# A hybrid streaming encoder layer: causal masks on DVE, and another order at the stage boundary, in the interleaved units and at the end

## The chip, the core and the metric

One core of a Trainium2 chip runs the whole layer as one program. The metric is the device time of one execution in microseconds (us). Five engines work side by side, each through its own queue in order: TensorE (PE, with its weight loads shown as PEld), VectorE (DVE), ScalarE (ACT), GpSimd (POOL) and SyncE (SP), which here issues all DMAs of the program.

## What is computed

One layer on 2048 prompt frames and 32 frames of a running stream with 512 cached rows, all in float32. A projection is split among two mixers: a state-space scan (SSD) and a forgetting attention (FoX) with 16 heads of 64. The attention part and the end are what the change touches:

```
def fox_attend(q, k, v, fq, fk, q_pos, k_pos):
    s = jnp.einsum('bqhd,bkhd->bhqk', q, k, preferred_element_type=jnp.float32) * ATTN_SCALE
    s = s + jnp.swapaxes(fq, 1, 2)[:, :, :, None] - jnp.swapaxes(fk, 1, 2)[:, :, None, :]
    s = jnp.where((k_pos[None, :] <= q_pos[:, None])[None, None], s, -jnp.inf)
    p = jax.nn.softmax(s, axis=-1)
    return jnp.einsum('bhqk,bkhd->bqhd', p.astype(v.dtype), v)
...
    y_attn = o.reshape(bsz, t, D_ATTN).astype(f32) * jax.nn.silu(z_attn.astype(f32))
    mixed = jnp.concatenate([y_ssm, y_attn], axis=-1).astype(x.dtype) @ w_out
    h = ALPHA * x.astype(f32) + mixed.astype(f32)
    ... layer norm of h
```

## The kernel before, in words

Products that need more than one pass of precision are made of a high and a low part (`hi`/`lo`, `xh`/`xl`, `yh`/`yl`), three matmuls for one product.

**Projections and SSD (until about 1384 us).** The input projection runs channel tile by channel tile. In its last part 24 jobs (8 each for q, k and z of the attention, list `jobs`) of five column blocks (`BL`) are interleaved with the steps of the SSD scan by `at(n, ...)`. Each block ends in `tile_q`, `tile_k` or `tile_z`, which write their results to DRAM (q and k as a high and a low half, z through SiLU). From here on the matmuls are held in program order (`strict`, `mm`).

**The boundary.** During the last job the SBUF of the SSD is given back (`sx.close()`), and `begin()` (at block `b == RB`) opens the pools of the next stage on the right side: `w_begin` loads the eight tiles of the output weight that the SSD half needs (`w_request`), and `more()` splits them into high and low (`w_split`). The rest of the last job's outputs go through tiles of the new pools (`ux`, `uh`, `ul`). When the last job is done the memory of the input is free, and the attention's pools are opened (`a0`, `aq`, `ap`).

**Attention, three streams in one.** For each of 8 head pairs `p` and 4 query blocks `g` of 512:

- the *max stream* (`maxima`): per step one block `r` of 128 queries against one block `c` of 512 keys, two heads; a matmul `mp<-k,qa`, and on DVE `tensor_tensor_reduce` (L725, `jk`), which takes the gate `fb` off and keeps the running maximum `mx`. In the diagonal block (`c == g`) a second matmul (`mp<-trq,idb`, bf16) adds the causal mask. Two PSUM buffers (`pmx`, `MB = 2`), shared with `turn` (`pm`, the transposed maxima) and `total` (`sum`).
- the *value stream* (`values`): per step `j` 128 keys against 512 queries, two heads: `s<-qa,k` and `s<-qb,k`, in the four diagonal steps a mask matmul `s<-trb,idb`, then the exponential on ACT (L791, `pr`), the running sum `acc` on POOL (L798), and two steps later the product with the values (`po<-pr,va`), every second step eight matmuls at once. There are 320 such steps, 128 of them diagonal.
- the *units* (`ssm_proj`): the SSD half of the output projection, 272 units of three matmuls (`u<-wh,uh` and two more). Eight units make one row of 128 frames; a row needs four tiles of 256 KB (`uh`, `ul`, a ring of `UB = 3` each).

The streams are woven by hand in the loop at the end of the stage: first `U0 = 8` units, then `L0 = 22` steps of the max stream with two units after each, then one value step at a time; after each value step come a max step, the `chores` (`turn`, `split`), the units that are due, a step of the sample stream and `finish_steps` (`total` and the rest of the normalisation of an earlier block).

**The end.** When the values are done, `finish_steps` closes the last block of the attention, while `products` starts on the attention half of the output projection with the first three tiles of frames (`first`); their rows 0 to 3 of eight are there early, 4 to 6 are requested with `rows`, row 7 needs the last block. Then tile 16 and tiles 3 to 15 follow; each has products, the residual, and a layer norm on DVE, ACT and POOL. `y_next` holds the split rows of the next tile.

What is not pinned or held by `strict` is placed by the scheduler of the tile framework, by priority and free buffers; `pin` keeps an instruction in program order on its queue.

Of the kernel before, what the change touches and what calls it, by code (L numbers as in the profile page):

```python
# [19 lines left out]
ND = 32  # L20
# [7 lines left out]
KB, K2B, VB, FB, QA, QB, L0, LEAD, U0, RB, S0 = 6, 4, 4, 4, 4, 3, 22, 22, 8, 2, 2  # L28
# [3 lines left out]
def hymba_step(  # L32
# [220 lines left out]
    def gates():  # L253
# [28 lines left out]
        one = g2.tile([16, 1], F32, name="one")  # L282
        V.memset(one, 1.0)
# [3 lines left out]
        def scan(out, d, initial=0.0):  # L287
            V.tensor_tensor_scan(out=out, data0=one.to_broadcast([16, out.shape[1]]), data1=d, initial=initial,
                                 op0=ALU.mult, op1=ALU.add)
# [72 lines left out]
    with tc.tile_pool(name="tp", bufs=2) as tp, tc.tile_pool(name="wt", bufs=2, side="right") as wtp:  # L362
        for i in range(8):
            hi, lo = load_w(w_tok[i], 256, wtp)
            if i == 7:
                w_first = load_w(w_ch[28], 128)
# [148 lines left out]
    k2t, ws, w_steps, w_raw = [], [], [], []  # L515
# [31 lines left out]

    def qt(kind, dtype=F32R):
        if len(qpool) == 1:
            return qpool[0].tile([128, TB], dtype, name=kind, bufs=1 if kind == "f" else 2)  # L550
        if kind == "f":
            return qpool[1].tile([128, 512], F32, tag="ux", name="ux", bufs=1)
        t = qpool[1].tile([128, 4, 128], F32R, tag="u" + kind, name="u" + kind, bufs=UB)
        return t.rearrange("p a b -> p (a b)")

    if True:
# [32 lines left out]
        jobs = [(i, fn, p) for p in range(8) for i, fn in [(2, tile_z), *qk]]  # L589
# [16 lines left out]
        def begin():  # L606
            ex = tc.tile_pool(name="ep", bufs=1, side="right")
# [3 lines left out]
            right.extend([ex, fx, wx, px])  # L611
            right.extend([x.__enter__() for x in (ex, fx, wx, px)])
            k2t.extend(right[4].tile([66, 2, 512], F32R, name=f"k2{i}") for i in range(K2B))
            for i in range(K2B):
                GP.memset(k2t[i][64:66].bitcast(F32), 1.0)
            qpool.append(right[6])
            w_begin(right[6])

        def more():
            for _ in range(3):  # L620
                next(w_steps[0], None)
# [3 lines left out]
        for j, (i, fn, p) in enumerate(jobs):  # L625
# [3 lines left out]
            for b, (t0, m) in enumerate(BL[::-1] if last else BL):  # L629
                if last and b == 1:  # L630
                    sx.close()
                if last and b == RB:
                    begin()
# [15 lines left out]
                if last and b >= RB:  # L649
                    more()  # L650
                at(n, ("use",))
# [17 lines left out]
    ex, fx, wx, px, ep, af, wq, pmx = right  # L669
    pa = p2.enter_context(tc.tile_pool(name="pa", bufs=1, space=PSUM))  # L670

# [3 lines left out]
    def load_k(p, c):  # L675
        cs = slice(512 * c, 512 * c + 512)
        k = a0.tile([128, 2, 512], F32R, tag="k", name="k", bufs=KB)
        S.dma_start(k[0:64].bitcast(F32), heads(kh_d[p][:, cs]))
        S.dma_start(k[64:128].bitcast(F32), heads(kl_d[p][:, cs]))
        return k  # L680

    def load_k2(p, c):
        k2 = k2t[(4 * p + c) % K2B]
        S.dma_start(k2[0:64].bitcast(F32), heads(kh_d[p][:, 512 * c:512 * c + 512]))
        return k2

    with tc.high_priority(offset=PO * OFF):
        k1 = load_k(0, 0)

    one = aq.tile([128, 32], F32, name="one")  # L690
    G.memset(one, 1.0)
# [4 lines left out]
    def load_v(p, c):  # L696
        va = ap.tile([128, 4, 128], F32, tag="va", name="va", bufs=VB)
        S.dma_start(va, v_d[p // 2][512 * c:512 * c + 512, 128 * (p % 2):128 * (p % 2) + 128]
# [3 lines left out]
    def load_f(p, c):  # L702
        fb = a0.tile([128, 2, 512], F32, tag="fb", name="fb", bufs=FB)
        S.dma_start(fb, fc_d[2 * p:2 * p + 2, 512 * c:512 * c + 512].unsqueeze(0).to_broadcast([128, 2, 512]))
        return fb

    def load_q(p, g):
        qa = a0.tile([128, 2, 512], F32R, tag="qa", name="qa", bufs=QA)
        for i in range(2):
            S.dma_start(qa[64 * i:64 * i + 64].bitcast(F32), heads(qh_d[p][:, 512 * g:512 * g + 512]))  # L710
        return qa

    def maxima(p, g, qa, ks, fbs, slot):
        mx = a0.tile([128, 2, 4, 4], F32, tag="mx", name="mx", bufs=2)
        for c in range(g + 1):
            for r in range(4):
                n = 512 if c < g else 128 * (r + 1)
                for hh in range(2):
                    ps = pmx.tile([128, 512], F32, tag="mp", name="mp")
                    mm(ps[:, 0:n], lhsT=qa[:, hh, 128 * r:128 * r + 128], rhs=ks[c][:, hh, 0:n],  # L720
                             start=True, stop=(c < g))
                    if c == g:
                        mm(ps[:, n - 128:n], lhsT=idb, rhs=trq, start=False, stop=True)
# [7 lines left out]
        def turn():  # L731
            qb = aq.tile([66, 2, 512], F32R, tag="qb", name="qb", bufs=QB)
            S.dma_start(qb[0:64].bitcast(F32), heads(ql_d[p][:, 512 * g:512 * g + 512]))
# [16 lines left out]

    chores, clock = [], [0]
# [9 lines left out]
    def values(p, g, qa, ks, slot, k2s, vas, mid):  # L761
# [15 lines left out]
        for j in range(nb):  # L777
# [5 lines left out]
            for hh in range(2):  # L783
# [3 lines left out]
                mm(ps[:, o], lhsT=k2s[j // 4][:, hh, js], rhs=qb[:, hh, o], start=False, stop=not diag)  # L787
# [3 lines left out]
                A.activation(pr[:, o], ps[:, o], AF.Exp, bias=fbi[:, g, j, h:h + 1])  # L791
                E = V if hh and (p, g) == (7, 3) else G
# [142 lines left out]
    def ssm_proj():  # L935
        loaded = []

        def load(i, q):
            if i >= 34:
                return  # L940
            t = i % 17
            L = 128 if t < 16 else ND
            for nm, d in (("uh", yh_d), ("ul", yl_d)):
                y = wq.tile([128, 4, 128], F32R, tag=nm, name=nm, bufs=UB)
                if L < 128:
                    G.memset(y.bitcast(F32), 0.0)
                S.dma_start(y[:, :, 0:L].bitcast(F32), d[t][:, 4 * q:4 * q + 4, 0:L])
                loaded.append(y)

# [10 lines left out]
        for q in range(2):  # L960
            load(0, q)
        yield
        for i in range(34):
# [4 lines left out]
            for k in range(8):  # L968
                if k % 4 == 0:
                    load(i + 1, k // 4)  # L970
# [16 lines left out]
    def max_stream():  # L987
        ks, fbs = [k1], [load_f(0, 0)]
        for i, (p, g) in enumerate(steps):
            if g < 3:  # L990
# [3 lines left out]
            qa, slot = load_q(p, g), []  # L994
# [7 lines left out]
    def val_stream():  # L1002
        k2s, vas = [load_k2(0, 0)], [load_v(0, 0)]
# [24 lines left out]
    ms = max_stream()  # L1028
# [14 lines left out]
    for i in val_stream():  # L1043
        if i is None:
            next(ms, None)
# [60 lines left out]
    with tc.tile_pool(name="op", bufs=1) as op, tc.tile_pool(name="p3", bufs=3, space=PSUM) as p3:  # L1106
# [82 lines left out]
        def weights():  # L1189
            if len(raws) > 1:  # L1190
                i = len(raws) - 2
                w3_split(raws[i], *more[i])
            if len(raws) < 8:
                raws.append(w3_request(*more[len(raws)]))

        weights()
        weights()
# [4 lines left out]
        for t in first[1:]:  # L1202
            for _ in range(3):
                weights()
            finish_steps()
            finish_steps()
            products(pss[t], ysf[t], range(4))
        yq = [rows(t, range(4, 7)) for t in first]
        w3_split(raws[6], *more[6])
        w3_split(raws[7], *more[7])  # L1210
        ready = [[]]
        for q in range(2):
            yr = w3.tile([128, 512], F32, tag="raw", name="yr", bufs=3).rearrange("p (k t) -> p k t", k=4)
            if q == 0:
                ready[0].append(y_request(16, yr, range(4)))
            else:
# [120 lines left out]
```

## Time and profile before

| what | value |
|---|---|
| median of 3 runs | 2716.4 us (2715.26 to 2716.52) |
| the profiled execution | 2715.73 us, its span 2714.0 us |
| granted TensorE clock, mean | 0.985 |
| ACT busy | 944.9 us (35%) |
| DMA | 379.70 MB, mean 140 GB/s |

The page sums up busy time by engine, groups of instructions by line, operation and tile, and the chain of work that ended last. A group's row has its count, its busy time in us, the mean duration in ns and the idle time of the engine just before its members, with who ended it. Matmuls are pipelined, so their durations overlap: what one costs is read from the starts in the timeline. In the stage windows the columns are the stretch, its length, then the busy time (and the count) of PE, PEld, DVE, ACT and POOL, the granted PE clock, the DMA share and GB/s.

### The profile page before, as it was taken

The numbers are of one execution on the slowest core, as the hardware profiler recorded it, in microseconds if no ns is written. First come the engines' busy times: TensorE is split into PE (matmuls) and PEld (weight loads), VectorE is DVE, ScalarE is ACT, GpSimd is POOL, SyncE is SP. The second block draws the span as 40 slices with busy tenths as digits, with TensorE's granted clock in tenths as the row PEclk, the third lists the DMA queues.
The fourth block names the chain that finished last, engine by engine and source line by source line (L and its number), as shares of the span: only waits on it lengthen the run. The fifth ranks groups of instructions, "written<-read, shape, count | busy, mean of one in ns | idle before, by whom it ended". The sixth has DMA issues, their size and how long they took to land. (4 is left out here: it accounts for less than half of the span.)

```text
span 2714.0 us, 41446 instructions
## 1 busy us (share of the span) xinstructions
PE 2588.5 (95%) x14469; PEld 2051.9 (76%) x14469; DVE 1210.5 (45%) x2813; ACT 944.9 (35%) x1919; POOL 1148.7 (42%) x993
## 2 busy tenths in 40 slices
PE   8999999999999999999948999999999999998798
PEld 8999999999999999999846555555555555554686
DVE  6876500000345444444214444445443434445687
ACT  4222211111344444444211444444444444443221
POOL 1011101010243344343310667777767676865344
PEclk9999999999999999999979999999999999999899
DMA  5221212232566666665485555555555656422564
GB/s 173 90 75 71 90 64 78 91 123 94 146 185 182 191 169 186 176 195 158 140 239 165 137 138 140 148 138 151 138 147 142 152 135 157 114 67 79 183 196 152
DMA packets 325753, 379.70 MB, mean 140 GB/s; under 512 B 61128, under 2 KB 216392, under 8 KB 325544
## 3 DMA queue, kind: packets, MB, share of 16 engines
q1 hardware_dynamic: 325544, 377.05, 49.6%
q8 instruction: 114, 1.87, 0.3%
q14 instruction: 95, 0.78, 0.1%
HBM read 242.83 MB, written 133.84 MB: 139 GB/s over the span
## 5 line engine op out<-in xcount | busy, mean ns | idle before, releaser
L798 POOL TENSOR_TENSOR acc<-acc,pr 128x512 f32<-128x512 f32 (+3 forms) x514 | 546.6, 1089 | 102.4 <-ACT pr L791 101.0
L80 PE MATMUL ps<-xh,w_hi 128*128 128x384 f32 (+2 forms) x1480 | 537.3, 363 | 7.1 <-ACT xh L148 5.7
L80 PE MATMUL ps<-xl,w_hi 128*128 128x384 f32 (+2 forms) x1480 | 517.8, 350 | 2.9 <-DVE xl L149 2.9
L80 PE MATMUL ps<-xh,w_lo 128*128 128x384 f32 (+2 forms) x1480 | 517.0, 350 | 0.0
L791 ACT ACTIVATE pr<-s,fbi 128x512 f32<-128x512 f32 (+3 forms) x640 | 365.8, 622 | 331.6 <-PE s L80 303.5
L725 DVE CUSTOM_DVE_ANT_0 jk<-mp,fb,mx 128x512 bf16<-128x512 f32 (+3 forms) x384 | 249.4, 650 | 309.8 <-PE mp L80 277.9
L373 PE MATMUL ps<-w_hi,xh 128*128 128x256 f32 x1088 | 300.8, 276 | 0.6 <-ACT o L380 0.6
L128 POOL TENSOR_TENSOR w_lo<-w_raw,w_hi 128x1024 fp32r<-128x1024 f32 x30 | 73.7, 2456 | 536.8 <-DVE w_hi L127 496.5
L375 PE MATMUL ps<-w_hi,xl 128*128 128x256 f32 x1088 | 300.7, 276 | 0.0
L374 PE MATMUL ps<-w_lo,xh 128*128 128x256 f32 x1088 | 300.6, 276 | 0.0
L80 PEld LDWEIGHTS ps<-xh,w_hi 128*128 128x128 f32 x1480 | 278.8, 188 | 28.3 <-issue 9.2
L80 PEld LDWEIGHTS ps<-xl,w_hi 128*128 128x128 f32 x1480 | 279.0, 189 | 23.0 <-issue 7.7
L80 PEld LDWEIGHTS ps<-xh,w_lo 128*128 128x128 f32 x1480 | 278.5, 188 | 12.5
L80 PE MATMUL po<-pr,va 128*64 128x512 f32 (+3 forms) x1280 | 271.0, 544 | 2.4 <-ACT pr L791 2.4
L725 DVE CUSTOM_DVE_ANT_0 jk<-mp,fb 128x512 bf16<-128x512 f32 (+3 forms) x256 | 164.2, 641 | 238.0 <-PE mp L80 198.1
L80 PE MATMUL s<-qa,k 128*128 128x512 f32 (+3 forms) x640 | 254.6, 398 | 3.6 <-ACT pr L791 3.6
L80 PE MATMUL s<-qb,k 66*128 66x512 f32 (+3 forms) x640 | 235.3, 368 | 0.0
L80 PE MATMUL mp<-k,qa 128*128 128x512 f32 (+3 forms) x640 | 221.0, 411 | 8.2 <-DVE mx L725 7.4
L373 PEld LDWEIGHTS ps<-w_hi,xh 128*128 128x128 f32 x1088 | 204.2, 188 | 0.8 <-ACT o L380 0.8
L80 PEld LDWEIGHTS mp<-k,qa 128*128 128x128 f32 x640 | 116.5, 193 | 116.2 <-issue 81.2
L375 PEld LDWEIGHTS ps<-w_hi,xl 128*128 128x128 f32 x1088 | 204.2, 188 | 0.0
L374 PEld LDWEIGHTS ps<-w_lo,xh 128*128 128x128 f32 x1088 | 204.2, 188 | 0.0
(220 smaller groups left out, 3954.8 us busy)
## 6 DMA issues: line engine op xcount, KB each, us to landing
w_raw<-in_w_ch SPq DMA_DIRECT2D x36, 512.0 KB
wt<-cs SPq DMA_DIRECT2D x32, 512.0 KB
k<-kh SPq DMA_DIRECT2D x64, 256.0 KB
fb<-fc SPq DMA_DIRECT2D x32, 512.0 KB
qa<-qh SPq DMA_DIRECT2D x64, 256.0 KB
uh<-yh SPq DMA_DIRECT2D x64, 256.0 KB
ul<-yl SPq DMA_DIRECT2D x64, 256.0 KB
xc<-ac SPq DMA_DIRECT2D x48, 192.0 KB
```

The source lines that it names most:

```text
L80: ins = T.matmul(*a, **k)
L128: G.tensor_tensor(out=lo[:, k:k + m, :], in0=r, in1=hi[:, k:k + m, :].bitcast(F32), op=ALU.subtract)
L373: T.matmul(ps, lhsT=xh[b][:, k, a], rhs=hi[:, k, :], start=(k == 0), stop=False)
L374: T.matmul(ps, lhsT=xh[b][:, k, a], rhs=lo[:, k, :], start=False, stop=False)
L375: T.matmul(ps, lhsT=xl[b][:, k, a], rhs=hi[:, k, :], start=False, stop=(k == 7))
L725: V.tensor_tensor_reduce(out=jk[:, 0:n], in0=ps[:, 0:n], in1=fbs[c][:, hh, 0:n], op0=ALU.subtract, op1=ALU.max, scale=1.0, scalar=-3.0e38 ...
L791: A.activation(pr[:, o], ps[:, o], AF.Exp, bias=fbi[:, g, j, h:h + 1])
L798: E.tensor_tensor(out=acc[:, hh, o], in0=acc[:, hh, o], in1=pr[:, o], op=ALU.add)
```

## The change

- **Masks.** The mask matmuls of both streams are taken out. In `maxima` the diagonal block is worked from `r = 3` down to 0, and before each `r` DVE takes the mask off the last 128 columns of the gate tile, both heads at once, in place. In `values` DVE takes the minimum of the diagonal 128 columns of `pr` and a tile `mkk` (3e38 where the key is allowed, 0 elsewhere) behind the exponential.
- **Boundary.** z is now the last of a head pair's three jobs. `begin()` comes one block earlier (`RB` 2 to 1), two weight splits per block instead of three; the first row of the units is requested in the last job (`load_rows`), its DMAs and those of the second row pinned; `k1`, `f1`, `q1` come next, and all loads of the attention (`load_dma`) are pinned until 16 max steps are done. `k2t` moves to the left side.
- **Units.** `L0` 22 to 16, one unit after each max step instead of two; six value steps then take an additional max step. In the loop the chores, the sample stream, `finish_steps` and the units now come before the max step.
- **End.** `finish_steps` twice before the first products; the rows 4 to 6 of each tile are requested right behind its first products; the residuals of two tiles earlier; rows two tiles ahead; the split of the next tile's rows ahead of the norm of the tile before.

The diff, cut to what matters:

```
-KB, K2B, VB, FB, QA, QB, L0, LEAD, U0, RB, S0 = 6, 4, 4, 4, 4, 3, 22, 22, 8, 2, 2
+KB, K2B, VB, FB, QA, QB, L0, LEAD, U0, RB, S0, C0 = 6, 4, 4, 4, 4, 3, 16, 22, 8, 1, 2, 16
...
+    def row_dma(*a):
+        ins = S.dma_start(*a)
+        if len(loaded) < 8:
+            pin(ins)
+
+    def load_rows(wq, i, q):
...
+            row_dma(y[:, :, 0:L].bitcast(F32), d[t][:, 4 * q:4 * q + 4, 0:L])
+            loaded.append(y)
...
-        jobs = [(i, fn, p) for p in range(8) for i, fn in [(2, tile_z), *qk]]
+        jobs = [(i, fn, p) for p in range(8) for i, fn in [*qk, (2, tile_z)]]
...
-            for _ in range(3):
+            for _ in range(2):
                 next(w_steps[0], None)
...
                 if last and b >= RB:
                     more()
+                    if b == 2:
+                        for q in range(2):
+                            load_rows(right[4], 0, q)
...
+    mkk = af.tile([128, 128], BF16, name="mkk")
+    VP.tensor_scalar(out=mkk, in0=trf, scalar1=0.0, scalar2=3.0e38, op0=ALU.is_equal, op1=ALU.mult)
...
+    def load_dma(*a):
+        ins = S.dma_start(*a)
+        if clock[0] < C0:
+            pin(ins)
...
-            for r in range(4):
+            for r in range(4) if c < g else range(3, -1, -1):
                 n = 512 if c < g else 128 * (r + 1)
+                if c == g:
+                    last = fbs[c][:, :, n - 128:n]
+                    V.tensor_tensor(out=last, in0=last, in1=trq.unsqueeze(1).to_broadcast([128, 2, 128]), op=ALU.subtract)
...
-                             start=True, stop=(c < g))
-                    if c == g:
-                        mm(ps[:, n - 128:n], lhsT=idb, rhs=trq, start=False, stop=True)
+                             start=True, stop=True)
...
-                if diag:
-                    mm(ps[:, c:c + 128], lhsT=idb, rhs=trb, start=False, stop=True)
                 pr = ap.tile([128, 512], F32, tag=f"pr{hh}", name="pr", bufs=PR)
                 A.activation(pr[:, o], ps[:, o], AF.Exp, bias=fbi[:, g, j, h:h + 1])
+                if diag:
+                    V.tensor_tensor(out=pr[:, c:c + 128], in0=pr[:, c:c + 128], in1=mkk, op=ALU.min)
...
     next(units)
+    k1 = load_k(0, 0)
+    f1 = load_f(0, 0)
+    q1 = load_q(0, 0)
+    ms = max_stream()
     for _ in range(U0):
         next(units)
         done += 1
-    for _ in range(L0):
+    for i in range(L0):
         next(ms)
+        if i == 4:
+            first = load_k2(0, 0), load_v(0, 0)
         clock[0] += 1
         do_chores()
-        for _ in range(2):
+        for _ in range(1):
             next(units)
             done += 1
...
         if i is None:
+            n += 1
+            clock[0] += 1
+            do_chores()
+            if n % 40 in (5, 9, 13, 17):
+                next(samples)
+            if n % FS == 0:
+                finish_steps()
+            while done < min(272, U0 + L0 + n * (272 - U0 - L0) // UG):
+                next(units, None)
+                done += 1
             next(ms, None)
             if lead < LEAD:
                 next(ms)
                 lead += 1
-            n += 1
-            clock[0] += 1
-            do_chores()
-            while done < min(272, 2 * L0 + U0 + n * (272 - U0 - 2 * L0) // UG):
-                next(units, None)
-                done += 1
-            if n % 40 in (5, 9, 13, 17):
-                next(samples)
-            if n % FS == 0:
-                finish_steps()
...
+        finish_steps()
         finish_steps()
         products(pss[0], ysf[0], range(4))
+        yq = [rows(0, range(4, 7))]
+        finish_steps()
+        split_next(2)
         finish_steps()
         finish_steps()
...
+        products(pss[1], ysf[1], range(4))
...
+        res = [residual_request(t) for t in first[:2]]
...
-            if i + 1 > TB0 and nxt is not None:
-                ready.append([rows(nxt, range(4 * q, 4 * q + 4)) for q in range(2)])
-            if nxt is not None:
+            if TB0 < i + 2 < len(order):
+                ready.append([rows(order[i + 2], range(4 * q, 4 * q + 4)) for q in range(2)])
+            if nxt is not None and len(res) < i + 2:
                 res.append(residual_request(nxt))
...
+            if i == 1 or i >= TB0 and nxt is not None:
+                y_next = [split(r) for r in ready.pop(0)]
             if out:
                 done = norm(*out)
                 store(out[0], *done)
             residual(t, *res[i])
-            if i + 1 >= TB0 and nxt is not None:
-                y_next = [split(r) for r in ready.pop(0)]
```

More of the change, by code (lines that the diff above doesn't have):

```diff
@@ L280, in gates @@
             S.dma_start(lf_o[:, d], s[q, o][0:16])
-        one = g2.tile([16, 1], F32, name="one")
-        V.memset(one, 1.0)
+        uni = g2.tile([16, 1], F32, name="uni")
+        V.memset(uni, 1.0)
         cl = g2.tile([16, 17], F32, name="cl")
@@ L287, in scan @@
         def scan(out, d, initial=0.0):
-            V.tensor_tensor_scan(out=out, data0=one.to_broadcast([16, out.shape[1]]), data1=d, initial=initial,
+            V.tensor_tensor_scan(out=out, data0=uni.to_broadcast([16, out.shape[1]]), data1=d, initial=initial,
                                  op0=ALU.mult, op1=ALU.add)
@@ L629, in hymba_step @@
             for b, (t0, m) in enumerate(BL[::-1] if last else BL):
-                if last and b == 1:
+                if last and b == RB:
                     sx.close()
-                if last and b == RB:
                     begin()
@@ L683, in load_k2 @@
         k2 = k2t[(4 * p + c) % K2B]
-        S.dma_start(k2[0:64].bitcast(F32), heads(kh_d[p][:, 512 * c:512 * c + 512]))
+        load_dma(k2[0:64].bitcast(F32), heads(kh_d[p][:, 512 * c:512 * c + 512]))
         return k2
[L687 to L691, printed above, removed]
+    k2t = [ep.tile([66, 2, 512], F32R, name=f"k2{i}") for i in range(K2B)]
+    for i in range(K2B):
+        GP.memset(k2t[i][64:66].bitcast(F32), 1.0)
     fbi = aq.tile([128, 4, 16, 16], F32, name="fbi")
@@ L1002, in val_stream @@
     def val_stream():
-        k2s, vas = [load_k2(0, 0)], [load_v(0, 0)]
+        k2s, vas = ([x] for x in first)
         for i, (p, g) in enumerate(steps):
@@ L1187, in hymba_step, with request, split_next @@
         raws, more = [], [(k, n) for k in range(4, 8) for n in range(2)]
[L1189 to L1197, printed above, removed]
+        def request():
+            raws.append(w3_request(*more[len(raws)]))
+        def split_next(m):
+            for _ in range(m):
+                w3_split(raws[cnt3[0]], *more[cnt3[0]])
+                cnt3[0] += 1
+                if len(raws) < 8:
+                    request()
+        cnt3 = [0]
+        for _ in range(3):
+            request()
+        finish_steps()
         finish_steps()
         products(pss[0], ysf[0], range(4))
+        yq = [rows(0, range(4, 7))]
+        finish_steps()
+        split_next(2)
         finish_steps()
         finish_steps()
[L1202 to L1216, printed above, removed]
-                ready[0].append(yr)
-        while late:
-            finish_steps()
+        products(pss[1], ysf[1], range(4))
+        split_next(1)
+        yq.append(rows(1, range(4, 7)))
+        finish_steps()
+        split_next(2)
+        products(pss[2], ysf[2], range(4))
+        yq.append(rows(2, range(4, 7)))
+        split_next(1)
+        finish_steps()
+        finish_steps()
+        split_next(2)
+        res = [residual_request(t) for t in first[:2]]
         ys = []
@@ L1223, in hymba_step @@
             products(pss[t], ys[t], range(4, 7))
+        while late:
+            finish_steps()
+        ready = [[]]
+        for t in first:
+            y_request(t, yq[t], (7,))
+        for q in range(2):
+            yr = w3.tile([128, 512], F32, tag="raw", name="yr", bufs=3).rearrange("p (k t) -> p k t", k=4)
+            ready[0].append(y_request(16, yr, range(4 * q, 4 * q + 4)))
         lg = op.tile([128, 1024], F32, name="lg")
```

78 lines of the change are left out of this document (35 added, 43 removed).

## The prediction

> **What bounds the kernel now.** I read the page's busy times first, then the stage windows, then who waited for whom on PE in the stages that are not full.
>
> ```profile
> PE 2588.5 (95%) x14469; PEld 2051.9 (76%) x14469; DVE 1210.5 (45%) x2813; ACT 944.9 (35%) x1919; POOL 1148.7 (42%) x993
> ```
> ```profile
> 1383.80:1421.80 38.00, 0.00 (x0) 0.00 (x0) 2.83 (x6) 5.10 (x9) 6.09 (x5) 0.56 1.05 256
> ...
> 1500.00:2400.00 900.00, 868.12 (x4162) 506.34 (x4162) 399.70 (x1223) 396.56 (x736) 650.75 (x647) 1.00 0.56 140
> ...
> 2478.00:2493.00 15.00, 8.61 (x36) 4.15 (x32) 12.81 (x14) 5.47 (x12) 8.19 (x7) 0.83 0.44 122
> 2493.00:2548.00 55.00, 39.46 (x150) 30.28 (x150) 25.25 (x43) 8.45 (x15) 11.15 (x8) 0.84 0.46 147
> 2548.00:2706.00 158.00, 155.84 (x670) 127.18 (x670) 136.50 (x157) 34.49 (x54) 73.99 (x29) 0.99 0.55 179
> ```
>
> PE bounds the kernel with 95%. In the attention (1500 to 2400) it is busy 868 of 900 us, DVE 44%, POOL 72%. It is empty for 38 us at the boundary, where the DMA engines are full (share 1.05, 256 GB/s), and for 15.5 of 55 us at the start of the end. The rest of the end is PE's again. So whatever leaves PE's stream in the attention is worth its full price as long as PE stays the bound, and two holes are there to be closed.
>
> **Masks out of PE.** In the timeline of PE, one diagonal value step (a start, a duration, the group):
>
> ```profile
> 1982.14 0.40 PE L80 MATMUL s<-qa,k 128*128 128x512 f32 x1
> ...
> 1983.79 0.39 PE L80 MATMUL u<-wh,uh 128*128 128x512 f32 x1
> 1984.02 0.40 PE L80 MATMUL u<-wl,uh 128*128 128x512 f32 x1
> 1984.26 0.39 PE L80 MATMUL u<-wh,ul 128*128 128x512 f32 x1
> 1984.49 0.34 PE L80 MATMUL s<-qa,k 128*128 128x384 f32 x1
> 1984.66 0.34 PE L80 MATMUL s<-qb,k 66*128 66x384 f32 x1
> 1984.84 0.23 PE L80 MATMUL s<-trb,idb 128*128 128x128 bf16 x1
> 1984.88 0.42 PE L80 MATMUL s<-qa,k 128*128 128x384 f32 x1
> 1985.14 0.34 PE L80 MATMUL s<-qb,k 66*128 66x384 f32 x1
> ...
> 1995.07 0.50 PE L80 MATMUL s<-qa,k 128*128 128x512 f32 x1
> ```
> ```profile
> L80 PE MATMUL s<-trb,idb 128*128 128x128 bf16 x256 | 59.4, 232 | 0.0
> L80 PE MATMUL mp<-trq,idb 128*128 128x128 bf16 x256 | 58.0, 230 | 0.0
> ```
>
> A mask's recorded 0.23 us is mostly overlap: the next matmul starts 0.04 us behind it (1984.84 to 1984.88). But that next matmul then holds PE for 0.26 us (1984.88 to 1985.14), where the same one without a mask ahead of it took 0.17 (1984.49 to 1984.66). I read the 0.09 as the weight load that is not hidden behind a mask. So a mask costs 0.13 us, and 512 of them 66 us. Two of eight value masks of a block stand ahead of the product with the values, which changes its tile shape anyway; for those 64 I count 0.04 only (less 6), and where a wait follows a mask the saving goes into the wait (less 2): **58 us**. Bounds: 20 us (512 x 0.04, if the follower's 0.09 stays) to 66.
>
> [...]
>
> **Masks into DVE.** 256 minima of 128x128 and 128 subtractions of 128x(2x128) come to DVE. The nearest rows:
>
> ```profile
> 1983.76 0.75 DVE L725 CUSTOM_DVE_ANT_0 jk<-mp,fb,mx 128x512 bf16<-128x512 f32 x1 [0.68 <-PE mp L80]
> ...
> 1984.66 0.75 DVE L725 CUSTOM_DVE_ANT_0 jk<-mp,fb,mx 128x512 bf16<-128x512 f32 x1
> ```
> ```profile
> 2471.79 0.68 DVE L798 TENSOR_TENSOR acc<-acc,pr 128x512 f32<-128x512 f32 x1
> ...
> 2475.91 1.77 DVE L798 TENSOR_TENSOR acc<-acc,pr 128x512 f32<-128x512 f32 x1
> ```
> ```profile
> 2525.10 0.29 DVE L933 TENSOR_TENSOR yl<-yr,yh 128x128 fp32r<-128x128 f32 x1 [0.17 <-ACT yh L932]
> ```
> ```profile
> L798 DVE TENSOR_TENSOR acc<-acc,pr 128x512 f32<-128x512 f32 x11 | 12.5, 1137 | 3.6 <-ACT pr L791 3.5
> ```
> ```profile
> L798 POOL TENSOR_TENSOR acc<-acc,pr 128x512 f32<-128x512 f32 x325 | 412.0, 1295 | 57.6 <-ACT pr L791 56.8
> ```
>
> The two `jk` of a max step take 0.90 us each with what belongs to them (1983.76 to 1984.66), 1.8 us a step. A 128x128 operation between SBUF tiles takes 0.29 us. But the same DVE add of SBUF tiles takes 0.68 us once and 1.77 another time, 1.14 in the mean of 11: up to 1.09 us, in the mean 0.46, are lost, about the length of one POOL add (1.30). I read that as DVE waiting for POOL's running instruction. A minimum thus costs m = 0.29 to 1.38 us, 0.75 at that mean. PE needs for four diagonal steps 12.9 us (1982.14 to 1995.07), 3.2 a step, about 2.9 without masks; DVE needs 1.8 + 2m. They are even at m = 0.55. I take m = 0.65, under the mean, because POOL's next add waits for the minimum itself and so often stands still; then DVE is 0.2 us too long in 128 steps: **26 us lost**. Bounds 0 and 212 us (m = 1.38). The subtractions lie in steps whose `jk` are narrower, and count in that bound. Behind a waiting minimum the `jk` are queued, for them the max matmuls wait (two PSUM buffers), behind those PE's whole stream. POOL's add and the product with the values also wait for the minimum, but come one to two steps later.
>
> [...]
>
> **The order in the loop.** Waits of PE in the attention (total, times, longest):
>
> ```profile
> PE pm L85 <- DVE mx L725: 14.3, 29, 0.6
> PE mp L80 <- DVE mx L725: 7.4, 18, 1.7
> PE sum L80 <- DVE mx L725: 6.4, 10, 0.7
> ```
>
> `pm` and `sum` need a PSUM buffer of the max matmuls issued just before. Behind the new order they come after the scores, a step later than the `jk` that free them, so these 20.7 us go. What is late next is the max step itself, behind ACT's copies of `pm` and `sum`, with two exponentials ahead of them in ACT's queue; the 0.7 us of a unit (1983.79 to 1984.49) cover part. I take **12 us gained**, bounds 0 and 20.
>
> **The boundary.**
>
> ```profile
> PE u L80 <- DMA out_kT<-ux: 38.1, 1, 38.1
> PE u L80 <- DMA uh<-yh: 6.6, 1, 6.6
> ```
> ```profile
> 1387.84 0.58 SPq L678 DMA_DIRECT2D k<-kh  x1
> ...
> 1411.98 0.34 SPq L947 DMA_DIRECT2D uh<-yh  x1
> ```
>
> The first unit's rows are issued at 1411.98, 28 us after PE ran dry, behind everything that SP could prefetch. With 38.1 + 6.6 us and some 3 us at the lower clock (0.56 in that window) this costs 48 us. After the change the weights and row 0 come in the last job, whose evictions also write one output instead of three, and eight units (5.6 us) run at once. `k1`, `f1`, `q1` (0.5 MB each by their tiles) still have to wait for the last job's memory, as `k<-kh` does at 1387.84: 1.5 MB at 256 GB/s are 6 us, so PE idles 2 to 4 us. The pinned loads of row 1 stand ahead of the second group's k, f and q and wait for units 4 to 7; the max steps of that group wait behind. Until the values start, two more groups (3 MB), three rows (3 MB) and 0.75 MB for the first values are due: 26 us of DMA against 16 x 0.7 us of units and 16 max steps of about 0.5, 19 us. So 7 more, and 2 of clock: 13 remain, **35 us gained**, bounds 20 and 43. That z is the last job changes nothing else: PE is full there. The 28 units not done early run later at the same price.
>
> **The end.**
>
> ```profile
> PE po L80 <- ACT yh L932: 14.3, 2, 9.1
> PE po L80 <- DVE yl L933: 1.3, 1, 1.3
> ```
>
> These 15.6 us are late rows (requested after the third tile's products) and a split queued behind a norm; both now come earlier, and some 3 us of low clock (0.84) go with them. Against it: `sum` now stands ahead of the first products and waits for the last adds, on a DVE that is busy 12.8 of 15 us there and gets eight minima of 0.3 to 1.4 us: 6 us. **12 us gained**, bounds 2 and 18. From 2548 on PE is full, so rows two tiles ahead bring nothing there.
>
> **The sum**, against the profiled execution's 2715.7 us (span 2714.0, 0.7 below the median of the runs): - 58 + 26 - 12 - 35 - 12 = - 91, **2625 us**.
>
> **The rivals.**
>
> 1. *DVE becomes the bound, slower.* If every minimum waits a whole POOL add (m = 1.38), 212 us are lost instead of 26: 2715.7 - 117 + 212 = 2811 us. It turns slower from m = 1.0 (128 x 0.9 = 117). For it: POOL is 72% busy, the add of 1.77 us. Against: the mean of 11 adds is only 0.46 over the bare one. 7%.
> 2. *DVE waits as in the mean* (m = 0.75, and the subtractions likewise where both diagonals meet): 51 us lost and more, 2650 to 2675 us. 18%.
> 3. *A mask is only its 0.04 us*, since the next weight load costs the same behind any matmul: 20 instead of 58, 2663 us. The 0.17 against 0.26 speaks against it. 8%.
> 4. *The boundary's hole moves but stays*: loads that aren't pinned (the sample stream's, the weights') go ahead again, or the pins don't reach the queue as meant, and the full DMA engines decide: 5 instead of 35 us, 2655 us. 10%.
> 5. *The gains and losses cancel*: 2%.
>
> **How the numbers follow.** The forecast has 55%. The low end takes the good bounds of boundary, end and loop and no stall on DVE, less what they hardly reach together: 2580. The high end takes in rivals 3 and 4 and all but the worst of rival 2, also together with a smaller gain at the end: 2685. Left out are rival 1, the cancelled case and the outermost of the rest, 17%. Faster by over 0.2% (5.4 us, about what a measurement can tell from none): 55 + 18 + 8 + 10 = 91%. Same 2%, slower 7%.
>
> **What would show it.** No mask groups on PE, and a step's second `s<-qa` as fast as its first. PE's waits for `mx` under `pm` and `sum` gone, and a new total under `mp<-DVE mx`: 10 to 50 us. The minimum's group on DVE at a mean of 0.5 to 0.8 us, of two kinds, bare and delayed. At the boundary units follow the last projection within 1 us, then waits for `k`, `qa` or `uh` of some 10 us. At the end no wait for `yh` over 2 us, one for `acc` before the first `po<-w3h`. I am wrong if the minimum's mean is near 1 us, or if PE still idles 30 us between the last job and the first scores.

## The result, and the profile after

The changed kernel takes 2746.6 us (2746.3 to 2748.4) against 2716.3 us (2715.3 to 2716.5) of the kernel before on the same chip: ratio 1.0114, 95% interval 1.0096 to 1.0131. It is slower by 1.1% where 2625 us and "faster" were forecast. The profiled execution has a span of 2746.7 us at a mean granted clock of 0.971 (before 0.985).

The page's busy times of the kernel after:

```profile
PE 2593.3 (94%) x13957; PEld 2047.9 (75%) x13957; DVE 1386.1 (50%) x3198; ACT 926.8 (34%) x1907; POOL 1161.5 (42%) x993
```

512 matmuls are gone, and yet PE is busy for longer (2593.3 us against 2588.5). Where the time went shows in the windows from the first to the last matmul of the scores, of before and of after (stretch, its length, busy PE, PEld, DVE, ACT, POOL, granted clock, DMA share, GB/s):

```profile
1483.90:2485.50 1001.60, 962.74 (x4609) 558.90 (x4609) 453.81 (x1330) 445.66 (x827) 721.89 (x711) 1.00 0.53 133
```
```profile
1448.90:2533.10 1084.20, 987.45 (x4211) 572.80 (x4209) 638.07 (x1724) 446.52 (x832) 736.07 (x709) 0.95 0.49 128
```

The stage of the values begins 35 us earlier and ends 48 us later: 82.6 us longer. PE's idle time in it rose from 38.9 to 96.8 us (+58), and by the clock of the row, rounded to 0.95, an estimated 0.05 x 1084 = 54 us more went into slower matmuls. About 23 us of work (28 units of 0.70 us and six max steps) were moved into it from before the first scores. Against these stand the masks, some 50 us (below). So the loss is stalls of PE, counted about twice: the wait, and the low clock behind it.

The boundary in both kernels, and PE's waits after, which answer to the rows for `pm`, `sum` and `mp` of before:

```profile
1384.00:1450.00 66.00, 20.63 (x78) 15.01 (x79) 9.62 (x30) 7.46 (x14) 5.89 (x5) 0.66 0.95 244
```
```profile
1384.00:1450.00 66.00, 37.43 (x116) 26.02 (x114) 26.55 (x80) 7.51 (x15) 8.90 (x11) 0.74 0.96 232
```
```profile
PE mp L80 <- DVE mx L758: 33.2, 52, 3.4
PE s L80 <- DMA qb<-mh: 17.3, 7, 3.9
PE mp L80 <- DMA qa<-qh: 16.4, 4, 5.8
PE pm L85 <- DVE mx L758: 15.0, 9, 2.9
```

At the boundary PE is idle for 28.6 instead of 45.4 us. In the attention, the 29 short waits of `pm` for DVE (0.6 at the longest) became 9 of up to 2.9 over the whole run, `mp` waits 33.2 instead of 7.4 us for DVE, and the wait for `qb<-mh` is new. The matmuls of the sample stream that use the same two PSUM buffers (`t_s` and `po_s`) wait 13.7 and 4.7 us for `mx`, where they waited 1.9 and 1.2 before. On DVE, the two new groups and the wait of the second:

```profile
L822 DVE TENSOR_TENSOR pr<-pr,mkk 128x128 f32<-128x128 f32 x256 | 124.5, 512 | 12.7 <-ACT pr L820 11.8
...
L752 DVE TENSOR_TENSOR fb<-fb,trq 128x256 f32<-128x256 f32 x128 | 90.3, 705 | 90.0 <-DMA fb<-fc 87.4
```
```profile
DVE fb L752 <- DMA fb<-fc: 87.4, 29, 8.7
```

The minimum's mean is 0.51 us, under the 0.65 of the forecast. What the forecast did not have is the wait of the subtraction: 29 times DVE stood still for a gate tile that was still on its way. The timeline of DVE and then of PE shows one of them:

```profile
1660.44 0.74 DVE L752 TENSOR_TENSOR fb<-fb,trq 128x256 f32<-128x256 f32 x1
1665.23 1.18 DVE L752 TENSOR_TENSOR fb<-fb,trq 128x256 f32<-128x256 f32 x1 [4.04 <-DMA fb<-fc]
1666.33 0.55 DVE L758 CUSTOM_DVE_ANT_0 jk<-mp,fb 128x384 bf16<-128x384 f32 x1
```
```profile
1663.63 0.39 PE L80 MATMUL s<-qb,k 66*128 66x512 f32 x1
1666.94 0.38 PE L85 MATMUL pm<-idf,mx 128*8 128x128 f32 x1 [2.92 <-DVE mx L758]
1666.97 0.78 PE L80 MATMUL u<-wh,uh 128*128 128x512 f32 x1
1667.55 0.63 PE L80 MATMUL u<-wl,uh 128*128 128x512 f32 x1
```

The subtraction of 1660.44 belongs to the block in work. The one of 1665.23 belongs to the last block of that head pair, three blocks ahead: the `jk` that needs it starts only at 1786.02, 121 us later. The subtraction isn't pinned and has no PE work ahead of it, so the scheduler puts it into DVE's queue as early as it likes: here before the `jk` of the current block. That tile's DMA was issued at 1658.72, since its ring (`FB = 4`) had no free buffer before; the last `jk` on the tile it replaces ended at 1657.70. DVE waits 4.04 us, `jk` behind it is late, `pm` finds no PSUM buffer, PE stands 2.92 us, and then a matmul of 128x512 takes 0.63 instead of 0.39 us.

### The profile page after: what moved, and what is told of

It reads as the page before. It is cut to its first block, busy times and chain, and to the rows that moved or that the text cites. A ratio compares the mean times of both kernels' runs of the same rounds, so it can differ in the third digit from the quotient of the medians.

```text
span 2746.7 us, 40723 instructions
## 1 busy us (share of the span) xinstructions
PE 2593.3 (94%) x13957; PEld 2047.9 (75%) x13957; DVE 1386.1 (50%) x3198; ACT 926.8 (34%) x1907; POOL 1161.5 (42%) x993
## 5 line engine op out<-in xcount | busy, mean ns | idle before, releaser
L829 POOL TENSOR_TENSOR acc<-acc,pr 128x512 f32<-128x512 f32 (+3 forms) x514 | 560.5, 1112 | 135.2 <-DVE pr L822 76.3
L80 PE MATMUL po<-pr,va 128*64 128x512 f32 (+3 forms) x1280 | 277.7, 552 | 3.4 <-DVE pr L822 3.3
L80 PE MATMUL mp<-k,qa 128*128 128x512 f32 (+3 forms) x640 | 219.7, 406 | 56.6 <-DVE mx L758 33.2
L80 PE MATMUL s<-qb,k 66*128 66x512 f32 (+3 forms) x640 | 242.5, 384 | 20.5 <-DMA qb<-mh 17.3
L80 PE MATMUL s<-qa,k 128*128 128x512 f32 (+3 forms) x640 | 244.3, 386 | 4.0 <-ACT pr L820 4.0
L80 PEld LDWEIGHTS mp<-k,qa 128*128 128x128 f32 x640 | 125.0, 199 | 146.3 <-DVE mx L758 69.8
```

Source lines behind the costliest of these rows:

```text
L80: ins = T.matmul(*a, **k)
L829: E.tensor_tensor(out=acc[:, hh, o], in0=acc[:, hh, o], in1=pr[:, o], op=ALU.add)
```

## The experiments

Theory 1: the early subtraction. Rivals: DVE has too much to do or POOL holds it up, whatever the order (2); the reorderings cost the time (3).

**Subtraction and `jk` in program order.**

```
-                    V.tensor_tensor(out=last, ..., op=ALU.subtract)
+                    pin(V.tensor_tensor(out=last, ..., op=ALU.subtract))
-                    V.tensor_tensor_reduce(out=jk[:, 0:n], ...)
+                    pin(V.tensor_tensor_reduce(out=jk[:, 0:n], ...))
```

> The changed kernel with one thing more: the subtraction from the gate tile and the running maximum (jk) are kept in program order on DVE. No operation is added or taken away. Theory 1 (the subtraction of a coming gate tile stands in DVE's queue ahead of jk of the current block and waits there for its DMA, with PE's max matmuls behind it): DVE's wait of 87.4 us for the tile falls under 15 us, PE's waits for mx (68 us over mp, pm, t_s, po_s in the profile after) fall under 25, and the time comes to 2660 to 2690 us. Theory 2 (DVE has too much to do, or is held up by POOL, whatever the order): within 8 us of the 2746.6 us. Theory 3 (the reorderings cost the time, the masks do not): within 8 us of 2746.6 as well.

**The reorderings alone**: both masks are matmuls of PE again, as before.

> The changed kernel with both masks as matmuls on PE again: the reorderings of boundary, units, loop and end alone. Theory 1: these are no loss; boundary and end have each gained about 16 us by the marks of the trace, and the loop's order some: 2665 to 2690 us. Theory 2: the same. Theory 3: the reorderings carry the loss, 2735 to 2775 us (2746.6 and up to 30 more, since the masks' gain goes).

**The minimum alone** (the maxima's mask on PE) and **the subtraction alone** (the values' mask on PE, the subtraction unpinned):

> The changed kernel with the mask of the maxima as a matmul on PE again and the minimum on DVE for the values kept. Theory 1 (the early subtraction is the loss): the minimum is harmless and takes 256 mask matmuls of up to 0.13 us off PE, so 10 to 35 us faster than the kernel with the reorderings alone. Theory 2 (256 minima of 0.51 us, and what POOL does to them, are too much for DVE): 10 to 60 us slower than that one. Theory 3: no difference to speak of between the kernels with and without DVE masks, all near 2746.

> The changed kernel with the mask of the values as a matmul on PE again and the subtraction from the gate tile on DVE kept, unpinned as in the change. Theory 1: it has the whole loss: 60 to 90 us slower than the kernel with the minimum alone, 2715 to 2760 us, and DVE waits 50 to 90 us for fb. Theory 2: DVE has 125 us less to do than in the changed kernel, so faster than the kernel with the minimum alone. Theory 3: near 2746 us like the others.

| kernel | us | ratio to before (95%) |
|---|---|---|
| subtraction and `jk` in order | 2724.1 (2713.5 to 2735.8) | 1.0035 (1.002 to 1.005) |
| reorderings alone | 2704.3 | 0.9960 (0.9945 to 0.9975) |
| with the minimum | 2703.7 | 0.9957 (0.9940 to 0.9974) |
| with the subtraction | 2752.2 | 1.0138 (1.0119 to 1.0158) |

The subtraction by itself costs 48 us against the matmuls it replaces, and the minimum neither costs nor brings anything that can be told from the spread. Both are less than was expected (60 to 90 slower, 10 to 35 faster), but theory 1 has the larger loss. DVE's wait for the tile falls with the order from 87.4 to 8.3 us; the row of the kernel in order:

```profile
L752 DVE TENSOR_TENSOR fb<-fb,trq 128x256 f32<-128x256 f32 x128 | 92.7, 724 | 10.2 <-DMA fb<-fc 8.3
```

But only 22.5 us came back instead of 57 to 87, and PE still waits 37.3 us at `mp` for DVE in that kernel. And the reorderings give 11 us (against 2715.5 of the kernel before, measured beside it) where the forecast had 59. Two more causes had to be found.

**The second cause: the chores.** In the kernel with the reorderings alone, PE stops for `qb` once in each of the last seven head pairs, at the first scores of `g = 3`, 16.5 us in all. One of these places, and the 20 us before and around it:

```profile
1662.28 0.39 PE L80 MATMUL s<-qa,k 128*128 128x512 f32 x1
1666.04 0.80 PE L80 MATMUL s<-qb,k 66*128 66x512 f32 x1 [3.37 <-DMA qb<-mh]
...
1667.27 0.63 PE L80 MATMUL u<-wl,uh 128*128 128x512 f32 x1
```
```profile
1640.00:1660.00 20.00, 19.91 (x104) 11.09 (x102) 6.41 (x26) 8.54 (x17) 17.12 (x17) 1.00 0.47 133
1660.00:1680.00 20.00, 16.63 (x64) 9.29 (x62) 5.71 (x16) 7.10 (x13) 7.85 (x7) 0.83 0.25 65
```

The wait takes 3.37 us, and by the granted clock of 0.83 the matmuls behind it lose another 0.17 x 20 = 3.4 us, an estimate: together about twice the length of the wait. (That 64 instead of 104 matmuls run comes in part from the shorter ones of the first stretch.) With the chores ahead of the max step, `turn` and `split` count their steps (`C1, C2 = 2, 3`) from a max step that stands later in its turn, so the maxima reach `qb` almost a step later. That is theory A. The edit: `C1, C2 = 1, 2`, in the kernel with the reorderings alone, in that with both masks on DVE in order, and in that with the minimum.

> The kernel with the reorderings alone (both masks on PE), and the two chores of a block one step earlier (C1, C2 from 2, 3 to 1, 2). Theory A: the new order in the loop put the chores a step later, so that the maxima reach qb late: 7 waits of PE for qb<-mh, 16.5 us, each followed by some microseconds at a lower granted clock (20-us stretches with 62 to 84 matmuls instead of some 95). Then the waits for qb go, the clock in the attention is back at 0.99 to 1.00, and the time falls by 25 to 40 us from 2704.3, to 2665 to 2680. Theory B (the lower clock comes from something else, and the wait for qb covers another one that is just as late): under 8 us of gain, 2696 to 2704.

> The changed kernel with the subtraction and jk in program order on DVE, and the chores one step earlier (C1, C2 = 1, 2). Theory A and theory 1 together: the 18 us of waits for qb and their clock go, on top of what the order on DVE brought: 2724.1 less 25 to 40, 2685 to 2700. If DVE's load (52% in the mean, with both masks) is what holds PE up, the waits for mx (37.3 us) grow by what the waits for qb gave: under 10 us of gain.

> The kernel with the minimum alone on DVE, and the chores one step earlier (C1, C2 = 1, 2). Theory A: 2703.7 less 25 to 40, 2664 to 2679. If the minimum's gain on PE (0.13 us x 256 = 33 us by the forecast) was hidden behind the waits for qb, it comes out now: 10 to 30 us below the kernel with the reorderings and early chores. If the minimum gives on DVE what it takes off PE: within 8 us of that kernel.

Measured: 2664.0 us (ratio 0.9802, 0.9788 to 0.9817), 2704.6 (0.9955, 0.9940 to 0.9970) and 2666.3 (0.9812, 0.9797 to 0.9826). The early chores bring 40 us, 19 and 37. With both masks on PE the waits for `qb` are gone and the stage is nearly full, 978 of 999 us:

```profile
1448.50:2447.90 999.40, 978.47 (x4709) 572.17 (x4707) 458.84 (x1355) 449.19 (x832) 719.75 (x711) 0.99 0.54 140
```

Theory A holds. But the minimum still gains nothing, and both masks on DVE, in order, are 41 us behind both on PE: there PE waits 44.9 us at `mp` for DVE between 1450 and 2500 us, with both masks on PE 12.3.

**What a mask on PE costs by itself**: the kernel before without the two mask matmuls (it leaves the causal mask out).

> The kernel before with the 512 mask matmuls taken out and nothing in their place (it leaves out the causal mask, so its output is another). It prices a mask on PE by itself. As forecast (0.13 us each, less what falls to waits): 58 us faster, 2658 us. If a mask costs no more than the 0.04 us to the next matmul's start: 2695 us. If the attention is bound elsewhere as soon as the masks are gone (DVE's and ACT's answers, PSUM buffers): in between, with more waits of PE for mx or pr than the 29 before.

2684.0 us (0.9878, 0.9861 to 0.9894): 32 us. In the stage:

```profile
1480.00:2455.80 975.80, 922.77 (x4117) 541.01 (x4117) 455.60 (x1329) 441.97 (x827) 720.03 (x711) 0.99 0.54 137
```

PE is busy 40 us less although the clock, as the rows round it, has fallen by 0.01 (10 us): an estimated 50 us for 512 masks, 0.10 us each. But its idle time rose by 14 to 53.0 us. So 24 of the 50 us went back into waits and clock, as in the third case of the expectation: PE waits 18.3 us at `mp` for DVE instead of 7.4.

**The third cause: POOL.** In the kernel with both masks on DVE in order and early chores, one subtraction takes 3.81 us, others 0.41. DVE, then POOL, then PE at that place:

```profile
1786.57 0.41 DVE L752 TENSOR_TENSOR fb<-fb,trq 128x256 f32<-128x256 f32 x1
...
1789.48 3.81 DVE L752 TENSOR_TENSOR fb<-fb,trq 128x256 f32<-128x256 f32 x1
1793.43 0.29 DVE L758 CUSTOM_DVE_ANT_0 jk<-mp,fb 128x128 bf16<-128x128 f32 x1
```
```profile
1789.37 0.50 POOL L777 TENSOR_TENSOR mh<-mr,mh 8x128 fp32r<-8x128 f32 x1
1789.83 1.27 POOL L876 TENSOR_TENSOR oz<-oz,z 128x512 f32<-128x512 f32 x1
1791.07 1.93 POOL L829 TENSOR_TENSOR acc<-acc,pr 128x384 f32<-128x384 f32 x2
```
```profile
1793.79 0.94 PE L80 MATMUL mp<-k,qa 128*128 128x512 f32 x2 [2.90 <-DVE mx L758]
```

POOL's row ends at 1793.00, the subtraction 0.29 us later: it stood for four POOL instructions one after another, and PE for 2.90 us. Another subtraction of that kernel, at 2070.70, took 3.82 us beside the same four POOL instructions, and the longest of the 128 took 3.835. Theory P is that, theory Q is DVE's load. The test leaves POOL's running sum out (a tile of ones in its place, so the attention isn't normalised), once with both masks on DVE and once with both on PE:

```
-                if j == 0 and g == 0:
-                    G.tensor_copy(acc[:, hh], pr)
-                elif j == 1 and g:
...
+                if j == 0:
+                    G.memset(acc[:, hh], 1.0)
```

> Both masks on DVE, subtraction and jk in program order, early chores (2704.6 us), and the running sum of the probabilities left out: POOL's adds go, a tile of ones takes their place, so the attention isn't normalised and the output is another. Theory P (a DVE operation between SBUF tiles stands until POOL's whole row of instructions is done, as the 3.81 us subtraction that ended with POOL's fourth instruction in a row, and jk and PE's max matmuls stand behind it): without POOL's adds the minima take 0.28 to 0.32 us, the subtractions 0.42 to 0.45, and the kernel is 25 to 45 us faster than its twin with both masks on PE, where it was 41 slower: 2615 to 2640. Theory Q (DVE's work and order, with or without POOL): still as slow as its twin or slower, 2655 to 2700.

> The twin of that: the reorderings with early chores and both masks on PE (2664.0 us), and the running sum left out in the same way. PE is full there with or without POOL's adds, so both theories expect 2652 to 2664.

2632.5 us against 2656.2: without POOL's adds the masks on DVE are 24 us faster (25 to 45 were expected), with them they were 41 slower. The two groups with POOL's adds (the kernel of 2704.6 us), and without them, when POOL is busy 22% instead of 43%:

```profile
L822 DVE TENSOR_TENSOR pr<-pr,mkk 128x128 f32<-128x128 f32 x256 | 126.7, 520 | 25.0 <-ACT pr L820 23.3
L752 DVE TENSOR_TENSOR fb<-fb,trq 128x256 f32<-128x256 f32 x128 | 97.6, 763 | 10.3 <-DMA fb<-fc 8.4
```
```profile
L822 DVE TENSOR_TENSOR pr<-pr,mkk 128x128 f32<-128x128 f32 x256 | 72.8, 303 | 33.3 <-ACT pr L820 30.7
L752 DVE TENSOR_TENSOR fb<-fb,trq 128x256 f32<-128x256 f32 x128 | 54.6, 427 | 10.2 <-DMA fb<-fc 8.4
```

0.30 and 0.43 us instead of 0.52 and 0.76. Theory P holds. Then the mask should go where POOL has no part: DVE adds it in the PSUM tile that `jk` reads next.

```
+                    if c == g:
+                        V.tensor_tensor(out=ps[:, n - 128:n], in0=ps[:, n - 128:n], in1=trq, op=ALU.add)
```

> The reorderings with early chores and the value mask on PE; the mask of the maxima is added by DVE in the PSUM tile that jk reads next (256 additions of 128x128) instead of being taken off the gate tile. It adds more instructions to DVE than the 128 subtractions did, at the same place. Theory P (the other side of DVE's delay is POOL's use of SBUF, and jk, which reads PSUM, was never held up): the addition takes the same time each, 0.2 to 0.35 us, and the kernel is 10 to 25 us below the one with both masks on PE: 2640 to 2654. Theory Q (any further work in front of jk holds PE up): 2664 to 2700.

2650.4 us (0.9756, 0.9742 to 0.9771), 14 us under the same kernel with this mask on PE, though DVE has 256 instructions instead of 128, at the same place:

```profile
L755 DVE TENSOR_TENSOR mp<-mp,trq 128x128 f32<-128x128 f32 x256 | 67.7, 296 | 168.5 <-PE mp L80 167.3
```

The kernel with the subtraction in order, early chores and the value mask on PE was not run, so the subtraction's own part of the 41 us is known only from the kernel with the minimum alone: that one is 2 us behind both masks on PE, which leaves some 38 us to the subtraction and its pins.

**Further runs.** The minimum left out of head pair 3, where DVE also prepares the second half of the output weight, and of the last block, where it adds up the running sum:

```
+        on_pe = p == 3 or (p, g) == (7, 3)
...
+                if diag and not on_pe:
```

> The kernel with the minimum alone and early chores (2666.3 us), but with the value masks on PE in head pair 3 and in the last block of pair 7, where by the starts of the scores it was 7 us and 7 us slower than the kernel with both masks on PE, while in most other pairs it was 1 to 3 us faster. If the minimum's loss lies where DVE also prepares the second half of the output weight and takes over the running sum: 2652 to 2658. If the losses only move to another pair: 2662 to 2668.

2657.5 us (0.9787, 0.9769 to 0.9805), 9 us less, as far as expected of a loss that lies in those two places; but the intervals of the two kernels overlap a little, so it is likely and not shown. The value mask, too, in PSUM, ahead of the exponential (`s` plus `trb` on DVE):

> Both masks added by DVE in PSUM: the maxima's in mp ahead of jk, the values' in s ahead of the exponential (instead of a matmul of PE in the kernel of 2650.4 us). Theory P: 256 more additions of some 0.26 us that POOL doesn't hold up, 256 matmuls less on PE at 0.08 us: 2630 to 2642. Theory R (now the exponential waits for DVE's queue, in which jk and the other additions stand, then pr, po and the s buffers are late): 2650 or more, with PE waiting for s buffers or pr.

2647.8 us (0.9738, 0.9722 to 0.9754; 2639.5 to 2648.4): 2.6 us, inside the spread and between the two theories, so the value mask gains little this way. The new order taken back in the loop alone, in the kernel with the reorderings alone (`C1, C2 = 2, 3`):

```
+            next(ms, None)
...
             n += 1
             clock[0] += 1
             do_chores()
...
-            next(ms, None)
```

> Both masks on PE, boundary, units and end as changed (C1, C2 = 2, 3), but in the loop the max step first and then chores, units, samples and finish_steps, as in the kernel before. If the new order in the loop, with its chores in time, gains the 12 us that the prediction gave it: 2676, against 2664.0 with the new order and early chores. If it gains the whole of what the marks of the two traces leave for it (values 2 us shorter, though some 25 us of units and max steps were moved into them): 2684 to 2692. If only the early chores matter: within 6 us of 2664.

2701.0 us (0.9945, 0.9929 to 0.9961). None of the three cases expected this. The new order as made is worth -3 us (2704.3), which is inside the noise, and with its chores in time 37 (2664.0). The old order with early chores was not run; it has only 1.9 us of waits for `qb` to lose. The chores alone, in the changed kernel:

> The changed kernel (both masks on DVE, the subtraction unpinned) with the chores one step earlier and nothing else. If the late chores and the early subtraction add up: 2746.6 less 38 to 40, 2707 us. If they hide one another (PE waits for qb while DVE waits for the gate tile): 2720 to 2745. The kernel with subtraction and jk in order was at 2704.6, so below that it can't come by much.

2750.5 us (1.0130, 1.0113 to 1.0147), no gain at all, and above both ranges that were expected:

```profile
DVE fb L752 <- DMA fb<-fc: 116.6, 31, 8.6
```

PE's waits for `qb` fall from 17.3 to 7.7 us, but DVE's for the gate tiles grow from 87.4 to 116.6, and with them PE's at `mp` from 33.2 to 57.5. So the two causes hid one another: order alone brings 22.5 us and early chores alone -4, both together 42. And one weight split per block of the last job instead of two, on the kernel of 2650.4 us:

> The kernel of 2650.4 us (the mask of the maxima added in PSUM) with one step of the weight splits per block of the last job instead of two. If the hole of 7 to 8 us ahead of the first unit comes from ACT's weight splits, which wait for their raw tiles ahead of the last evictions: it falls under 3 us, and the time by 3 to 6 us, unless the units then wait for their weights. If the DMA engines decide (share 0.95): the hole moves to the waits for weights, k and qa, and the time stays within 3 us.

2648.4 us (0.9748, 0.9733 to 0.9762), 2 us less, which is inside the noise. Before, ACT's weight splits stood ahead of the last evictions, and the first unit waited 7.4 us; now it waits 0.6, and the units wait for their weights instead:

```profile
PE mp L80 <- DMA qa<-qh: 11.9, 2, 6.4
PE u L80 <- DVE wh L97: 7.2, 2, 6.9
```

So the hole moves, as expected if the DMA engines decide (their share from 1384 to 1450 us is 0.98 here, and 0.93 to 0.97 in eight other kernels with the changed boundary). Last, both masks in PSUM, the last block's value mask on PE, and one split per block:

> What came out best, together: both masks added by DVE in PSUM (2647.8 us), but the value mask on PE in the last block of pair 7, and one weight split per block at the boundary (2 us below its twin). By the starts of the scores the last pair should take 106 us instead of 108.7 and the others what they took with both masks in PSUM: 2641 to 2646. If the waits for qb (6.1 us) that came with both masks in PSUM grow, nothing is gained: 2646 to 2650.

2646.8 us (0.9736, 0.9720 to 0.9752): 2.6% under the kernel before and 3.6% under the changed one. From the kernel of 2647.8 us it can't be told apart.

## Why the prediction was wrong

The failed step is "Masks into DVE", in its sentence "The subtractions lie in steps whose `jk` are narrower, and count in that bound". It priced the subtraction by its length. Its place in the queue, its DMA and POOL beside it were not asked for. In its place the runs showed 48 us of loss by the subtraction alone: DVE waits 87 us for gate tiles, in the case shown 121 us before the tile is needed, and PE behind it. A second step, "The order in the loop", left out the chain from `pm` to `qb`, which costs 40 us with both masks on PE.

| step | forecast | measured |
|---|---|---|
| masks out of PE | -58 | -32 alone; 26 of it in the stage, whose stream is 50 shorter and gives 24 back |
| masks into DVE | +26 | minimum with its matmuls gone: -1; subtraction likewise: +48 |
| order in the loop | -12 | +3 as made, -37 with the chores in time |
| boundary | -35 | about -13 |
| end | -12 | -15 |
| sum | -91 | +30 |

In the measured column the first row stands for itself, since the second holds what both streams lose and gain; -1 + 48 + 3 - 13 - 15 are +22, and 8 of the 30 us are left. By whole kernels the account closes: the reorderings together bring 11 us, and both masks on top of them cost 42.

- *Masks out of PE.* The price of a mask, 0.11 us in the sum, was nearly right (0.10). That 0.09 us of it is a weight load was the author's reading; no run took it apart. Wrong was that all of the price would reach the end.
- *The minimum* was forecast at -29 + 26, next to nothing, and is at -1, with early chores at +2. That is partly luck: half of the 32 us that both masks bring by themselves is 16, which leaves about 15 as the price of the minimum, so both terms were too large. POOL's part in it was seen, but bounded by one add of POOL (1.38 us); in order and with early chores, the longest subtraction took 3.835 us. Rivals 1 and 2 had the mechanism of the third cause, and looked for the loss mostly in the minimum, where little of it lies.
- *The subtraction.* +48 us with its 256 matmuls gone, which are worth up to 25. In the changed kernel its order gives back 22.5, and 42 together with early chores. What then still separates both masks on DVE from both on PE, 41 us, comes with POOL's adds, by the runs without them.
- *The loop.* "a step later than the `jk` that free them" is what happened to `pm` and `sum`, and in the kernel with the reorderings alone their waits went. But the same step delays what hangs on `pm`: `turn`, `split`, a DMA and `qb`. The prediction named ACT's copies as what is late next, and did not follow the chain to its reader. Its bound of 20 was too low as well: mended, the order brings 37, more than the 20.7 us of waits that were to go; where the rest comes from was not taken apart.
- *The boundary.* The stretch from the last projection's matmul to the first scores went from 100.2 to 64.2 us, but 23 of these 36 us are work put off. The first unit came 7.5 us after the last projection, where the prediction named 1 us. Rival 4 had the kind: by the run with one weight split the hole only moves. That the loads that aren't pinned hold the DMA engines is argued, and which of them counts most was not tried.
- *The end* came as forecast: 228.5 us from the last scores before, 213.6 after. It was not taken apart, so its terms are not confirmed by that.
- *The signs.* Two of the signs that the prediction gave for itself came although the kernel was slower: the minimum's mean of 0.51 us and the 33.2 us at `mp`. Of its signs of being wrong, one nearly came: PE idles 28.6 us between 1384 and 1450, where it named 30.

Open: with the boundary, units and end as changed and the old order in the loop, the stage takes 1034.1 us:

```profile
1450.10:2484.20 1034.10, 988.40 (x4709) 578.02 (x4709) 457.62 (x1356) 449.80 (x832) 719.72 (x711) 0.99 0.53 134
```

That is 32.5 more than before, 23 of them moved work. The other 9, about the 8 of the sum that are left, may be partly the clock (0.99); what causes them, no run tells.

## What to carry to other kernels

Before an operation goes to another engine, ask where the scheduler will put it in that engine's queue and what it waits for there: an instruction that only waits for a load, with no work of the busy engine ahead of it, can be put blocks ahead of its use and hold up everything behind it (here three blocks and 121 us, with a wait of 4.04 us on DVE and 2.92 on PE). Whatever is moved a step later has a reader; follow its chain to the end, and try the mends together, since two stalls can hide one another (22.5 and -4 us alone, 42 together). Where POOL works on SBUF beside it, a mask for a tile that the matmul has just written can be added in PSUM, next to its reader: for the maxima that was the cheapest of the three ways tried (2650.4 us against 2664.0 with the mask on PE), for the values it gained little (2.6 us).

## What the runs showed of the hardware

- **DVE stood for a whole row of POOL's instructions.** An operation of DVE between SBUF tiles stood 3.4 us longer than its 0.41, through four POOL instructions, not one; three of 128 took 3.81 to 3.835 us in the kernel of 2704.6 us, while half took 0.43 us or less. `jk`, which reads one tile in PSUM and the gate in SBUF, took at most 753 ns in the changed kernel and in that of 2704.6 us (744 in the median of its 384 with `mx` in the changed kernel, 750 in order), and the additions in PSUM took 0.296 us in the mean of 256, with POOL busy for 719 of the 988 us of that stage.
- **A stall of PE cost about twice its length,** by the estimate above for the kernel with the reorderings alone: 3.37 us of wait, and 3.4 at the granted clock of 0.83. The matmuls of 128x512 behind it took 0.63 instead of 0.40 us for some microseconds. So they did in the same kernel behind a wait of 1.82 us, but only from a second wait of 0.79 us on:

```profile
1933.33 0.50 PE L80 MATMUL s<-qb,k 66*128 66x512 f32 x1 [1.82 <-DMA qb<-mh]
1933.68 0.40 PE L80 MATMUL s<-qa,k 128*128 128x512 f32 x1
...
1935.44 0.80 PE L80 MATMUL mp<-k,qa 128*128 128x512 f32 x1 [0.79 <-DVE mx L757]
...
1936.46 0.63 PE L80 MATMUL s<-qb,k 66*128 66x512 f32 x1
```

  In the attention of the kernel before, waits of up to 1.39 us left the clock of their 20 us at 1.00; behind one of 1.66 us, with another of 0.34 us 0.8 us later, it was 0.91.
